# The output projection of the pooling channels as seven block products, inside the last attention pass of a transformer block on one NeuronCore

## The chip, the cores and the metric

The kernel runs on one core of a Trainium2 chip. The core has a matrix engine (PE; PEld is its loading of weights), a vector engine (DVE), an activation engine (ACT), GpSimd (POOL) and a queue engine (SP) which here issues nearly all transfers. The kernel puts PE's results into PSUM, in banks of 128 x 512 fp32 numbers, and all else into SBUF; GpSimd works on SBUF alone here. The metric is the time of one execution in device microseconds; a smaller number is better. Traces give, for one profiled execution, the start and the duration of every instruction.

## The reference, cut to what matters

```python
for layer in range(DEPTH):                                    # DEPTH = 1, S = D = 1024
    h = rmsnorm(x, norm1_g[layer])
    proj = h @ w_in[layer]                                    # q | k | v | f_logit | u
    attn = forgetting_attention(q, k, v, log_f)               # 8 heads x 64, causal: 512 channels
    pool = multiscale_pool(u, w_pool[layer], pool_scale[layer])   # 4 groups x 128: 512 channels
    mixed = concatenate([attn, pool], axis=-1)
    x = x + mixed @ w_out[layer]                              # the output projection, 1024 x 1024
    h2 = rmsnorm(x, norm2_g[layer])
    x = x + (silu(h2 @ w_gate[layer]) * (h2 @ w_up[layer])) @ w_down[layer]
return rmsnorm(x, final_g)
```

The output projection contracts over 1024 mixed channels, in eight chunks of 128: chunks 0 to 3 are the pairs of attention heads, chunks 4 to 7 the four pooling groups. All data is fp32. The kernel writes each operand as a high and a low part in a rounded fp32 format and computes a product as three matmuls (high x high, high x low, low x high).

## The kernel before, in words

**Stages.** First comes RMSNorm, the input projections and the pooling (to about 100 us in the trace), then four passes of attention over two heads each (to about 350 us), the last rows of the output projection with the second norm and its transposes (to about 410 us), then the gate and up products (to about 820 us) and the down products with the final norm. The gate, up and down products are already written as seven block products instead of eight.

**Attention with a filler.** `attend` (L711) runs one pass of eight jobs. A job is one head and two blocks of 128 queries; its steps are scores (`z`, L617 and L618), transposes of the scaled probabilities (`tp`, L643) and products with the values (`po`, L657). Scores are made one job ahead. ACT takes the exponential (L626), and GpSimd divides by the row sum (`p`, L629). Behind each step `attend` takes some steps from a generator, the filler, so that PE has other matmuls between those that wait for a softmax. In passes 0, 1 and 2 the filler is the projection of the next heads (`project`, `project_v23`); in pass 3 it is the output projection. The instructions are recorded in this order, and the framework's scheduler then sets each engine's own order; each engine runs its list strictly in order.

**The output projection before.** `first_rows` (L817) makes, for each of eight row blocks `tt` and each half of the columns, one PSUM group over chunks 4 and 5 (`rows2`, L803: six matmuls, then a DVE add into the row of x held in SBUF, L811). `second_rows` (L844) does the same over chunks 6, 7 and 0 (nine matmuls). Chunks 1, 2 and 3 come last (`last_row`, L873), when the last heads are done; chunk 3 is `mix_halves` (L859), which reads the last pair of heads back from DRAM in halves. Every chunk needs two pages, 128 x 1024 each: the mixed channels (`mixd` in DRAM, transposed) and the rows of `w_out`. A page is loaded (`raw_page`, L750, most into one of the two buffers `wr`), and split (`split`, L119): ACT writes the high part, DVE or GpSimd the low part. The groups use two PSUM banks with the tag `m` in turn. The rows of x are loaded whole, 128 x 1024 (`x2_load`, L794).

**Buffers that the change touches.** `vc` in `vpool` holds the pooled features of two groups (`pf01`, L505) until they are split, and values of the third head pair from pass 1 on. `va` holds values that the last job still reads, and takes the raw half pages of chunk 3. `hi` (two buffers of 128 x 512) serves `project`.

## Time and profile before

| what | value |
|---|---|
| time, median of 3 runs | 1035.73 us (1035.46 to 1036.53) |
| the profiled execution, first to last instruction (its own time is given as this span) | 1033.6 us |
| PE busy | 1024.3 us, 5104 matmuls |
| DVE, ACT, POOL busy | 632.8, 454.2, 381.1 us |
| mean granted TensorE clock | 0.998 |
| moved by DMA | 130.21 MB |

The span is what the trace covers; 2.1 us of the median lie outside it. A busy share of PE says little by itself, since consecutive matmuls overlap: the start-to-start distance of two matmuls is what one costs. In a row of a timeline stand the start and the duration in us, the engine, the line, the operation, the output and inputs, and the shapes. "o" is a PSUM group of the output projection, "r_mix" and "r_wo" are raw pages, "h_" and "l_" (or "hl_") their high and low parts.

### The profile page before, as it was taken

To read this page: it belongs to the slowest core of one execution; us is meant where nothing else is said; L and a number is where in the kernel's file an instruction comes from. 1 tells how busy PE (TensorE), PEld (TensorE's weight loads), DVE (VectorE), ACT (ScalarE), POOL (GpSimd) and SP (SyncE) were. 2 spreads that over 40 slices of the span, in tenths; PEclk is the share of its full clock that TensorE was granted. 3 is DMA by queue.
4 is the path that set the end of the run, shared out by engine and by line. 5 is a ranking of instruction groups with operands and counts; after the bars stand their busy time and mean duration, and the time that the engine had idled before them with its cause. 6 is when DMAs were issued, how large, how long until landed. Compare 5 with 4: busy or idle time off the path is not lost.

```text
span 1033.6 us, 14202 instructions
## 1 busy us (share of the span) xinstructions
PE 1024.3 (99%) x5104; PEld 868.9 (84%) x5104; DVE 632.8 (61%) x1000; ACT 454.2 (44%) x733; POOL 381.1 (37%) x312
## 2 busy tenths in 40 slices
PE   9999999999999999999999999999999999999997
PEld 7988888998888888888888888888888888888886
DVE  7565566776886479744433334334334789788886
ACT  7434355665665257533333233233233343333346
POOL 4350121213346043447537536636637510000045
PEclk9999999999999999999999999999999999999999
DMA  7224434333643134343143143143236755353424
GB/s 251 53 47 143 105 81 103 84 102 89 224 175 106 49 136 129 103 143 112 62 132 113 62 133 112 64 131 113 81 113 251 248 204 175 110 198 97 153 92 163
DMA packets 108439, 130.21 MB, mean 126 GB/s; under 512 B 7369, under 2 KB 70353, under 8 KB 108369
## 3 DMA queue, kind: packets, MB, share of 16 engines
q1 hardware_dynamic: 96544, 108.18, 33.4%
q10 hardware_dynamic: 11504, 20.47, 5.2%
q8 instruction: 40, 0.66, 0.2%
q0 software_dynamic: 320, 0.66, 0.2%
q14 instruction: 31, 0.25, 0.1%
HBM read 86.29 MB, written 33.03 MB: 115 GB/s over the span
## 4 chain that ended last, share of the span: by engine, by line
PE 98%; DMA 1%; ACT 0%; DVE 0%; POOL 0%; issue 0%; ACTq 0%; POOLq 0%
PE gu_P L161 14%; PE gu_P L162 14%; PE gu_P L163 14%; PE d L161 7%; PE d L162 7%; PE d L163 7%; PE po L657 4%; PE tp L643 3%; PE o L161 3%; PE o L162 3%; PE qk L161 3%; PE qk L162 3%; PE qk L163 3%; PE o L163 3%; PE v L374 2%; PE z L618 2%
## 5 line engine op out<-in xcount | busy, mean ns | idle before, releaser
L121 DVE TENSOR_TENSOR gu_P_l<-s,gu_P_h 128x1024 fp32r<-128x1024 f32 (+1 forms) x48 | 66.5, 1393 | 98.6 <-ACT gu_P_h L120 98.5
L162 PE MATMUL d<-d,d 128*128 128x512 f32 (+1 forms) x308 | 119.5, 388 | 0.0
L163 PE MATMUL d<-d,d 128*128 128x512 f32 (+1 forms) x308 | 119.5, 388 | 0.0
L629 POOL TENSOR_SCALAR p<-p,rr 128x128 f32<-128x128 f32 (+3 forms) x64 | 48.6, 764 | 175.5 <-DVE rr L628 140.2
L161 PE MATMUL d<-d,d 128*128 128x512 f32 x308 | 107.8, 388 | 0.0
L120 ACT ACTIVATE d<-r_f 128x1536 fp32r<-128x1536 f32 (+1 forms) x28 | 38.8, 1384 | 117.6 <-PE d L162 101.6
L121 DVE TENSOR_TENSOR gu_P_l<-r,gu_P_h 128x1024 fp32r<-128x1024 f32 x32 | 48.9, 1527 | 64.3 <-ACT gu_P_h L120 64.3
L1063 POOL TENSOR_TENSOR s<-r 128x1024 f32<-128x1024 f32 x10 | 24.0, 2401 | 161.9 <-DMA r<-in_w_up_dram 116.0
L120 ACT ACTIVATE gu_P_h<-r 128x1024 fp32r<-128x1024 f32 x32 | 33.8, 1060 | 91.1 <-PE gu_P L162 35.5
L162 PEld LDWEIGHTS d<-d,d 128*128 128x128 f32 x308 | 57.8, 188 | 12.0 <-DVE d L121 0.2
L161 PEld LDWEIGHTS d<-d,d 128*128 128x128 f32 x308 | 57.8, 188 | 12.0
L163 PEld LDWEIGHTS d<-d,d 128*128 128x128 f32 x308 | 57.8, 188 | 11.9
L626 ACT ACTIVATE p<-p,mn 128x128 f32<-128x128 f32 (+3 forms) x64 | 49.3, 772 | 32.8 <-DVE mn L620 29.9
L1291 POOL TENSOR_SCALAR sse<-sse 128x1 f32<-128x1 f32 x7 | 3.5, 494 | 158.1 <-ACT junk L1287 158.1
L1150 POOL TENSOR_TENSOR h<-h,qh 128x512 f32<-128x512 f32 x33 | 44.3, 1345 | 32.3 <-ACT qh L1148 24.1
L648 DVE TENSOR_TENSOR tl<-tp,th 128x512 fp32r<-128x512 f32 (+1 forms) x80 | 49.3, 632 | 10.7 <-ACT th L647 9.7
L120 ACT ACTIVATE gu_P_h<-s 128x1024 fp32r<-128x1024 f32 (+1 forms) x48 | 47.0, 984 | 19.7 <-PE gu_P L162 13.0
L1147 DVE TENSOR_TENSOR qh<-gu_P,sn_sU 128x512 f32<-128x512 f32 x22 | 15.2, 690 | 60.5 <-POOL h L1150 43.2
L121 DVE TENSOR_TENSOR d<-r_f,d 128x1536 fp32r<-128x1536 f32 (+1 forms) x28 | 45.7, 1633 | 10.5 <-ACT d L120 10.5
L163 PE MATMUL qk<-hTh,l_qk 128*128 128x512 f32 x128 | 50.7, 396 | 0.0
L161 PE MATMUL qk<-hTh,h_qk 128*128 128x512 f32 x128 | 50.6, 395 | 0.0
L162 PE MATMUL qk<-hTl,h_qk 128*128 128x512 f32 x128 | 50.4, 394 | 0.0
(337 smaller groups left out, 3067.1 us busy)
## 6 DMA issues: line engine op xcount, KB each, us to landing
r_f<-hsdP SPq DMA_DIRECT2D x77, 256.0 KB
r_wd<-in_w_down_dram SPq DMA_DIRECT2D x22, 512.0 KB
hsdP<-f ACTq DMA_DIRECT2D x43, 256.0 KB
r<-in_w_gate_dram SPq DMA_DIRECT2D x21, 512.0 KB
r<-in_w_up_dram SPq DMA_DIRECT2D x21, 512.0 KB
s<-hi SPq DMA_DIRECT2D x64, 128.0 KB
hsdP<-h ACTq DMA_DIRECT2D x32, 256.0 KB
x<-in_x_dram SPq DMA_DIRECT2D x8, 512.0 KB
```

The costliest lines, as they stand in the source:

```text
L120: mark["hi"] = nc.scalar.activation(out=hi, in_=src, func=AF.Copy)
L121: return eng.tensor_tensor(out=lo, in0=src, in1=f32(hi), op=ALU.subtract)
L161: nc.tensor.matmul(ps, lh, rh, start=start, stop=False, **kw)
L162: nc.tensor.matmul(ps, lh, rl, start=False, stop=False, **kw)
L163: mark["mm"] = nc.tensor.matmul(ps, ll, rh, start=False, stop=stop, **kw)
L626: nc.scalar.activation(out=pr[:, :n], in_=pr[:, :n], func=AF.Exp, scale=-1.0, bias=mn, accum_out=rs)
L629: nc.gpsimd.tensor_scalar(out=pr[:, :n], in0=pr[:, :n], scalar1=rr, scalar2=1.0, op0=ALU.mult, op1=ALU.mult)
L643: nc.tensor.transpose(tp[:, w : w + P], probs[h, 2 * sb + a][:, s * P : (s + 1) * P], ident)
L648: nc.vector.tensor_tensor(out=tl[:, :w], in0=tp[:, :w], in1=f32(th[:, :w]), op=ALU.subtract)
L657: mark["pv"] = nc.tensor.matmul(po[:, first * P : 2 * P], vt[p][:, s, j, :], part[:, o : o + wd], start=(s == 0 and part is th), stop=(s = ...
L1063: g(out=s1, in0=a21, in1=a22, op=ALU.add)
L1150: nc.gpsimd.tensor_tensor(out=h, in0=h, in1=q, op=ALU.mult)
```

## The change

The four pooling chunks (a contraction over 512) are taken as a 2 x 2 block product: 512 tokens by 256 channels, times 256 channels by 512 columns. Seven products of sums of blocks replace eight. The four sums on each side are made by GpSimd during passes 0 and 1 from `mixd` and `w_out` in DRAM and stored in DRAM again (`sumd`), in four rounds through the buffer `vc`: two loads of 512 KB, four subtractions or additions of 128 x 512, one store of 1 MB. `project_v23` first finishes what is left of these rounds.

In pass 3 the filler is `output_steps`: chunk 0 alone for four rows, then P2 with chunk 0, then P7 and P4, then P1, P6, P5 and P3, each for two token blocks in two PSUM banks. A chain of products keeps adding to its bank, and after each product DVE adds the running sum to the half row of x that it belongs to. Fourteen pages take the place of eight; three later pages (`LATE`) go through the two small buffers `hi` in halves, and rows of x are loaded in halves. A step has 6 or 9 matmuls as before; there are 30 steps instead of 32, and `attend` takes 25 of them instead of 27.

```diff
-    def project_v23():
+    def project_v23(side):
+        for _ in side:
+            pass
         vtile(2)
...
-    def attend(p, fill, counts, drain=True):
+    def attend(p, fill, counts, drain=True, side=iter(())):
...
                 for f in step:
                     f()
+                next(side, None)
                 want = quota * (k + 1) // len(steps)
...
+    rounds = [("wo", 0), ("wo", 1), ("mix", 0), ("mix", 1)]
+    def quarter_load(r):
+        kind, i = rounds[r]
+        t = quarters[r] = vpool.tile([P, 4, 512], F32, tag="vc", bufs=1, name=f"quarters{r}")
+        for k in range(2):
+            dst = t[:, 2 * k : 2 * k + 2, :].rearrange("p a e -> p (a e)")
+            nc.sync.dma_start(out=dst, in_=page_source(kind, NPAIR + 2 * k + i))
+    def quarter_sums(r):
...
+        for out, in0, in1, op in todo:
+            nc.gpsimd.tensor_tensor(out=out, in0=in0, in1=in1, op=op)
+            yield
+            yield
+    def quarter_store(r):
+        nc.sync.dma_start(out=sumd[rounds[r]], in_=quarters[r])
...
+    def part(ps, k, c, start, stop):
+        (ah, al), (bh, bl) = operands["mix", k], operands["wo", k]
+        for i in range(2):
+            ts, hs = slice(i * 512 + c * P, i * 512 + (c + 1) * P), slice(i * 512, (i + 1) * 512)
+            mm3(ps, ah[:, ts], al[:, ts], bh[:, hs], bl[:, hs], start and i == 0, stop and i == 1, True)
...
+    SPLITS = [
+        ("mix", "P2", M, G, -1), ("wo", "P2", O, V, 0), ("mix", "P7", M, G, 2), ("wo", "P7", O, V, 3),
+        ("mix", "P4", ST1, G, 5), ("wo", "P4", VC, V, 6), ("mix", "P1", M, G, 8), ("wo", "P1", O, V, 9),
+        ("mix", "P6", M, G, 12), ("wo", "P6", O, G, 13), ("mix", "P5", ST0, G, 14), ("wo", "P5", W, V, 15),
+        ("mix", "P3", ST1, G, 16), ("wo", "P3", VC, G, 18), ("wo", 1, O, V, 24), ("mix", 1, M, G, 24),
+        ("wo", 2, O, V, 26), ("mix", 2, M, G, 27), ("wo", 3, W, V, 30),
+    ]
...
+        def link(k, down, right, start, stop, more=False):
+            def do(c):
+                ps = fresh(f"o{k}", c) if start else held[c]
+                part(ps, k, c, start, stop and not more)
+                tt = c + down * NH
+                if more:
+                    whole(ps, tt, right, False, stop)
+                add_to(tt, right, ps)
...
+        order = [(alone, 0), (alone, 1)]
+        order += chain(("P2", 0, 0, True, True, True))
+        order += chain(("P7", 1, 1, True, False), ("P4", 1, 0, False, True, True))
+        order += chain(
+            ("P1", 0, 0, True, False), ("P6", 1, 0, False, False), ("P5", 1, 1, False, False),
+            ("P3", 0, 1, False, True, True),
+        )
...
-    attend(3, fill, [3, 3, 4, 4, 4, 4, 3, 2], drain=False)
+    attend(3, fill, [2, 3, 4, 3, 4, 4, 3, 2], drain=False)
```

In `SPLITS` the columns are the page, the destination, the engine of the low part (G is GpSimd, V is DVE) and the step ahead of which the split is recorded.

**Where the order moves, first place: GpSimd at the start of attention.** `p0_0` is the first head's first block of probabilities; `quarters0` and `quarters1` are the first two rounds of sums. Before:

```order
L432 DMA augd_101<-clo_831 8x1024
L432 DMA augd_101<-nlo_839 8x1024
L629 TENSOR_SCALAR p0_0_1205<-p0_0_1205,rr0_0_1213 128x128
L629 TENSOR_SCALAR p0_1_1216<-p0_1_1216,rr0_1_1224 128x256
L629 TENSOR_SCALAR p0_2_1258<-p0_2_1258,rr0_2_1266 128x384
```

And after:

```order
L432 DMA augd_101<-nlo_839 8x1024
L770 TENSOR_TENSOR quarters0_1240<-quarters0_1240 128x512 x4
L770 TENSOR_TENSOR quarters1_1479<-quarters1_1479 128x512 x3
L631 TENSOR_SCALAR p0_0_1209<-p0_0_1209,rr0_0_1217 128x128
L631 TENSOR_SCALAR p0_1_1220<-p0_1_1220,rr0_1_1228 128x256
L631 TENSOR_SCALAR p0_2_1265<-p0_2_1265,rr0_2_1273 128x384
L770 TENSOR_TENSOR quarters1_1479<-quarters1_1479 128x512
```

Seven sums stand ahead of the first scaling of probabilities; in SP's list the store of the first round and the loads of the second stand among the copies of the key stacks of the first heads.

**Second place: GpSimd in the second half of the last pass.** `p7_i` are the last head's blocks, `l_...` the low parts of pages. Before:

```order
L629 TENSOR_SCALAR p7_3_3963<-p7_3_3963,rr7_3_3971 128x512
L121 TENSOR_TENSOR hl_mix0_3900<-r_mix0_3666,hl_mix0_3900 128x1024
L121 TENSOR_TENSOR l_mix1_3983<-r_mix1_3980,h_mix1_3982 128x1024
L629 TENSOR_SCALAR p7_4_4044<-p7_4_4044,rr7_4_4057 128x640
L121 TENSOR_TENSOR l_wo2_3989<-r_wo2_3986,h_wo2_3988 128x1024
L121 TENSOR_TENSOR l_mix2_3995<-r_mix2_3992,h_mix2_3994 128x1024
L629 TENSOR_SCALAR p7_5_4094<-p7_5_4094,rr7_5_4107 128x768
L629 TENSOR_SCALAR p7_6_4150<-p7_6_4150,rr7_6_4163 128x896
L121 TENSOR_TENSOR l_wo3_4001<-r_wo3_3998,h_wo3_4000 128x1024
L629 TENSOR_SCALAR p7_7_4190<-p7_7_4190,rr7_7_4203 128x1024
```

After:

```order
L631 TENSOR_SCALAR p7_3_4042<-p7_3_4042,rr7_3_4050 128x512
L121 TENSOR_TENSOR l_mixP6_3996<-r_mixP6_3862,h_mixP6_3995 128x1024
L121 TENSOR_TENSOR l_woP6_4026<-r_woP6_3913,h_woP6_4025 128x1024
L631 TENSOR_SCALAR p7_4_4101<-p7_4_4101,rr7_4_4114 128x640
L121 TENSOR_TENSOR l_mixP5_4054<-r_mixP5_3999,h_mixP5_4053 128x1024
L631 TENSOR_SCALAR p7_5_4151<-p7_5_4151,rr7_5_4164 128x768
L121 TENSOR_TENSOR l_mixP3_4118<-r_mixP3_4057,h_mixP3_4117 128x1024
L121 TENSOR_TENSOR hl_woP3_4167<-r_woP3_4080,hl_woP3_4167 128x1024
L631 TENSOR_SCALAR p7_6_4204<-p7_6_4204,rr7_6_4217 128x896
L631 TENSOR_SCALAR p7_7_4243<-p7_7_4243,rr7_7_4256 128x1024
L121 TENSOR_TENSOR l_mix1_4370<-r_mix1_4170,h_mix1_4369 128x1024
L121 TENSOR_TENSOR l_mix2_4415<-r_mix2_0_4403,h_mix2_4414 128x512
```

The low parts of the pages of P6, P5 and P3 stand where those of chunks 0, 1, 2 and 3 stood, and chunks 1 and 2 come behind the last scaling.

**Third place: SP at the end of attention.** `at7_i` are results of the last head on their way to `mixd`. Before:

```order
L669 DMA mixd_100<-at7_2_4233 64x256
L865 DMA r_mix3_4326<-mixd_100 128x512
L669 DMA mixd_100<-at7_3_4311 64x256
L865 DMA r_mix3_4326<-mixd_100 128x512
L992 DMA r_gu0_P1_4428<-in_w_gate_dram 128x4x128
```

After:

```order
L671 DMA mixd_100<-at7_2_4285 64x256
L988 DMA r_mix3_4380<-mixd_100 128x512
L820 DMA r_mix2_0_4403<-mixd_100 128x512
L820 DMA r_mix2_1_4404<-mixd_100 128x512
L671 DMA mixd_100<-at7_3_4357 64x256
L988 DMA r_mix3_4380<-mixd_100 128x512
L820 DMA r_wo3_0_4420<-in_w_out_dram 128x512
L820 DMA r_wo3_1_4421<-in_w_out_dram 128x512
L1117 DMA r_gu0_P1_4494<-in_w_gate_dram 128x4x128
```

The loads of chunk 2's mixed page and of chunk 3's weights, which were issued during the pass before, stand between and behind the two loads of chunk 3's mixed page.

160 lines of the change are left out of this document (112 added, 48 removed).

## The prediction, made before the changed kernel was run

> **What bounds the kernel now.** I read the page first: busy shares, the chain, the granted clock.
>
> ```profile
> span 1033.6 us, 14202 instructions
> PE 1024.3 (99%) x5104; PEld 868.9 (84%) x5104; DVE 632.8 (61%) x1000; ACT 454.2 (44%) x733; POOL 381.1 (37%) x312
> PEclk9999999999999999999999999999999999999999
> PE 98%; DMA 1%; ACT 0%; DVE 0%; POOL 0%; issue 0%; ACTq 0%; POOLq 0%
> ```
>
> PE is the chain from end to end at an undiminished clock. But matmuls overlap, so a busy PE could still be waiting inside its durations. The busy times by stage, with the count of matmuls in brackets, and one stretch of the timeline settle that:
>
> ```profile
> core 0: us, PE busy (x) PEld busy (x) DVE busy (x) ACT busy (x) POOL busy (x), PEclk, DMA share, GB/s
> 270.00:275.00 5.00, 5.00 (x30) 4.38 (x29) 5.00 (x16) 3.31 (x7) 1.01 (x1) 1.00 1.02 381
> 275.00:300.00 25.00, 25.00 (x152) 22.21 (x152) 21.23 (x54) 15.97 (x33) 11.68 (x10) 1.00 0.67 235
> 300.00:325.00 25.00, 25.00 (x151) 22.00 (x149) 19.67 (x51) 18.80 (x36) 18.48 (x14) 1.00 0.37 116
> 425.00:800.00 375.00, 375.00 (x1656) 310.50 (x1655) 151.54 (x143) 127.79 (x168) 207.87 (x112) 1.00 0.35 116
> ```
>
> ```profile
> 282.47 0.51 PE L643 MATMUL tp<-ident,p 128*128 128x128 f32 x3
> 282.73 0.48 PE L161 MATMUL o<-h_wo,hl_mix 128*128 128x512 f32 x1
> 283.06 0.39 PE L162 MATMUL o<-l_wo,hl_mix 128*128 128x512 f32 x1
> 283.28 0.39 PE L163 MATMUL o<-h_wo,hl_mix 128*128 128x512 f32 x1
> ```
>
> In the gate and up stage 1656 matmuls take 375 us: one of 512 columns costs 0.2264 us start to start, though its duration reads 0.39. In the last attention pass the projection's matmuls start 0.22 to 0.23 us apart as well. Only the first after a group of transposes takes longer, 0.33 us (282.73 to 283.06), 0.10 more. So PE is at its own pace in the pass that is changed, and each matmul taken away is worth its 0.2264 us, as long as no operand is late. The question is then only what the change makes late.
>
> **The change, part by part.** I sum against the span, 1033.6; the 2.1 us by which the median exceeds it should stay.
>
> *Matmuls.* Chunks 4 to 7 took 4 chunks x 16 groups x 3 = 192 matmuls; seven products of 2 chunks x 4 token blocks x 3 make 168. 24 x 0.2264 = **-5.4 us**. The changed order also enters the projection's matmuls from transposes or scores 19 times instead of 27; at 0.10 us each that is up to -0.8. Not every entry need cost as much as the one shown, so I take **-0.3** and keep 0 and -0.8 as ends.
>
> *GpSimd's sums.* Four rounds of four operations. Nearest rows: an operation of the same size on GpSimd, and the idle time of GpSimd ahead of its first scaling.
>
> ```profile
> L1150 POOL TENSOR_TENSOR h<-h,qh 128x512 f32<-128x512 f32 x33 | 44.3, 1345 | 32.3 <-ACT qh L1148 24.1
> 115.55 1.49 POOL L629 TENSOR_SCALAR p<-p,rr 128x128 f32<-128x128 f32 x3 [38.96 <-DVE rr L628]
> ```
>
> 16 x 1.345 = 21.5 us, of which seven operations, 9.4 us, stand in the 39 us in which GpSimd idled. What they wait for is a chain through SP: load, four sums, store of the round, load of the next. Its start and what stands behind it:
>
> ```profile
> 93.80 1.22 DVE L121 TENSOR_TENSOR pl<-pf,ph 128x1024 fp32r<-128x1024 f32 x1
> 95.68 0.76 SPq L549 DMA_DIRECT2D s<-augd  x2
> 105.95 0.47 SPq L569 DMA_DIRECT2D s<-hi  x1
> 119.68 0.27 PE L643 MATMUL tp<-ident,p 128*128 128x128 f32 x1
> ```
>
> The buffer `vc` is free at 95.0, SP at 96.4. A load of 256 KB takes 2.4 to 3.0 us from issue to use (rows below, at the end of attention); 1 MB has 0.75 MB more at 381 GB/s (window 270:275), 2.0 us, so about 4.7. Load until 101.2, sums until 106.6, store until 111.3, second load until 116.0, three sums until 120.0, two scalings in 0.9 (the first three took 1.49): 120.9. The first transpose was at 119.68; the changed order puts seven more projection matmuls ahead of it, so it is due at 121.3. That fits by 0.4 us. The store also stands ahead of the key copies that were issued at 105.95; these slip by about 1 us, with the first scores moved back by the same 1.6. I take **+0.3** for the start; ends 0 and +3 (each of the three transfers 1 us slower). The later rounds meet probabilities that are scaled a whole job ahead: GpSimd waits for PE to free their buffers, not the reverse.
>
> ```profile
> POOL p L629 <- PE tp L643: 15.2, 3, 7.4
> ```
>
> *Pages of the last pass.* Fourteen pages for eight, three later ones in halves. Costs by group:
>
> ```profile
> L121 POOL TENSOR_TENSOR l_mix<-r_mix,h_mix 128x1024 fp32r<-128x1024 f32 x4 | 9.6, 2402 | 7.5 <-ACT h_mix L120 7.5
> L121 DVE TENSOR_TENSOR l_mix<-r_mix,h_mix 128x1024 fp32r<-128x1024 f32 x1 | 1.2, 1223 | 0.0
> L120 ACT ACTIVATE h_wo<-r_wo 128x1024 fp32r<-128x1024 f32 x6 | 6.3, 1058 | 2.6 <-DMA r_wo<-in_w_out_dram 2.6
> L811 DVE TENSOR_TENSOR x_r<-o,x_r 128x512 f32<-128x512 f32 x16 | 10.7, 680 | 4.1 <-PE o L163 4.1
> ```
>
> Of the six more pages' worth, three low parts go to GpSimd (7.2 us) and about three to DVE (3.7 us), and ACT gets 6 x 1.06 = 6.4 us at most. The windows leave 3.8 to 9 us idle in 25 on each, so on average there is room: **0**. The densest place is five low parts (12.0 us) and four scalings between the end of P7 and the first product of P3: there the changed order has 132 matmuls, 21.7 us at the 152 in 25 of the window. Six pages go through two raw buffers in that time; one takes load 2.4 + ACT 1.06 + GpSimd 2.4 = 5.9 us, two at a time 2.95, six 17.7. Slack 4.0 us.
>
> *Running sums in two banks.* PE may add to a bank again only after DVE's add has read it. With steps of six, the other bank's step gives 1.36 us; the add takes 0.68. Cover enough: **0**; if DVE is held by a page's low part (1.22), 0.5 us at a time. The 32 adds themselves are as many as before. The loads of x in halves carry the same bytes, behind fewer others: 0.
>
> *The end of attention.* Here the change puts transfers in series where before they were done. The rows of before, by engine:
>
> ```profile
> 349.85 0.28 PE L657 MATMUL po<-tl,v 128*128 128x128 f32 x1
> 358.21 0.39 PE L161 MATMUL o<-h_wo,h_mix 128*128 128x512 f32 x1
> 359.57 0.39 PE L161 MATMUL o<-h_wo,mix_h 128*128 128x512 f32 x1
> ```
>
> ```profile
> 350.16 0.33 SPq L865 DMA_DIRECT2D r_mix<-mixd  x1
> 351.03 0.87 SPq L669 DMA_DIRECT2D mixd<-at  x1
> 353.39 0.33 SPq L865 DMA_DIRECT2D r_mix<-mixd  x1
> ```
>
> ```profile
> 353.12 0.63 ACT L120 ACTIVATE mix_h<-r_mix 128x512 fp32r<-128x512 f32 x1 [2.57 <-DMA r_mix<-mixd]
> 355.83 0.63 ACT L120 ACTIVATE mix_h<-r_mix 128x512 fp32r<-128x512 f32 x1 [2.07 <-DMA r_mix<-mixd]
> ```
>
> ```profile
> 353.84 0.69 DVE L121 TENSOR_TENSOR mix_l<-r_mix,mix_h 128x512 fp32r<-128x512 f32 x1 [0.86 <-ACT mix_h L120]
> ```
>
> Call V the end of the last product with the values, 349.97 here. Before, 36 matmuls cover the loads of chunk 3 (last rows from V + 8.2, chunk 3 used at V + 9.6), whose first half is split by V + 4.6: 5 us of slack. After, 30 matmuls follow V, so the last rows start at V + 6.9 and want chunk 3's weights at V + 8.3. These are now late: SP's list is chunk 3 (V + 0.2), two halves of chunk 2 (V + 0.6, V + 1.0), the last result's store, chunk 3 again, then the two halves of the weights, which need the `hi` buffers that chunk 2 leaves. Chunk 3's first half can be split at V + 3.2 (350.16 to 353.12), chunk 2's behind it by V + 4.4 and V + 5.0 (0.63 each), GpSimd's low parts (half of 2.40) end at V + 5.6 and V + 6.8, the weights' first half is there 2.4 to 3.0 later, V + 8.0 to 8.6, its high part at V + 8.7 to 9.2. PE waits 0.4 to 0.9: **+0.6**. The second half's high part comes at V + 9.9 to 10.4, eight matmuls (1.8) after PE resumes at 8.9: in time. Ends: 0, if both loads are quicker by 0.4; +2.5, if each of the two loads in series takes 0.6 more and each of two low parts another 0.65. What is late next is nothing more: the second norm and its transposes follow the last rows as before.
>
> [...]
>
> ```profile
> 278.35 1.71 DVE L121 TENSOR_TENSOR l_wo<-r_wo,h_wo 128x1024 fp32r<-128x1024 f32 x1
> 276.57 2.40 POOL L121 TENSOR_TENSOR l_mix<-r_mix,h_mix 128x1024 fp32r<-128x1024 f32 x1 [3.24 <-ACT h_mix L120]
> 278.95 2.10 POOL L629 TENSOR_SCALAR p<-p,rr 128x1024 f32<-128x1024 f32 x1
> ```
>
> A DVE low part that usually takes 1.22 took 1.71 where it began inside a GpSimd low part that ended at 278.97, and the scaling behind it took 2.10. [...]
>
> **Sum.** -5.4 - 0.3 + 0.3 + 0.6 = -4.8: span 1028.8, median 1035.7 - 4.8 = **1030.9 us**.
>
> **Rivals.** *A. Attention's start comes late.* The chain of transfers through SP has 0.4 us to spare and seven sums ahead of the first scaling. For it: GpSimd and SP go strictly in order. Against: the scores themselves are moved back. At +1.5 to 3 instead of 0.3: 1032.1 to 1033.6.
>
> [...]
>
> *C. The filler was cover, not load.* The last pass loses 18 matmuls, 4.1 us, ahead of V; if the heads' own chain (score, exponential, scaling, transpose) cannot go faster, PE waits that long and the change does not give what it takes away: -5.4 - 0.3 + 0.9 + 4.1 = -0.7, 1035.0. Against it: probabilities lie a job ahead, and DVE and ACT have idle time in the windows.
>
> *D. Slower: the ring of two raw buffers.* Place: between the end of P7 and P3. If a page costs 5.2 us there instead of 2.95 (loads and splits hardly overlapping, as SP, ACT and GpSimd each go in order among stores, exponentials and scalings), six take 31.2 against 21.7, 9.5 us late: 1030.9 + 9.5 = 1040.4. It costs from 3.6 us a page and makes the kernel slower from 4.8. For it: GpSimd is 18.48 of 25 us busy there already. Against: with two buffers the transfers of one overlap the splits of the other, and DMA is at a share of 0.37 there.
>
> **How the numbers follow.** Forecast 0.56, A 0.12, B 0.12, C 0.11, D 0.09. The forecast's own range is 1029.8 (all stalls 0, -0.5 us of entries more or less) to 1032. I give **1029.3 to 1034.6**: it leaves out D, about half of C and a little below. Two runs of this kernel can be told apart at about 0.2%, 2.1 us: faster means below 1033.7, slower above 1037.8. Faster: 0.56 + 0.10 (A) + 0.10 (B) + 0.02 (C) = 0.78; slower: D, 0.09; same: the rest, 0.13.
>
> **What would show it.** PE's count falls to 5080, and in 425:800 nothing changes but the place. [...] A P3 product waiting for `hl_wo` by microseconds would show D. A gain above 6.2 us would show that I missed something that PE waited for before.

## The result and the profile after

The changed kernel takes 1044.95 us (1041.50 to 1046.48) against 1036.13 us (1035.46 to 1037.70) for the kernel before: a ratio of 1.0082 (95% interval 1.0062 to 1.0102). It is slower by 8.8 us, 0.8%, clear of the noise; the prediction had it 4.8 us faster.

The page of the changed kernel, its head, PE's clock and PE's waits:

```profile
span 1039.7 us, 14286 instructions
PE 1023.7 (98%) x5080; PEld 864.0 (83%) x5080; DVE 636.0 (61%) x1005; ACT 460.9 (44%) x742; POOL 410.5 (39%) x332
PEclk9999999999999999999999999999999999999999
```

```profile
PE po L659 <- DVE at L670: 1.5, 2, 1.2
PE o L161 <- ACT h_wo L120: 1.2, 1, 1.2
PE warm L254 <- DVE junk L252: 1.2, 1, 1.2
PE tr_a L150 <- DVE x L300: 0.9, 1, 0.9
PE qk L161 <- ACT p L628: 0.9, 1, 0.9
PE po L659 <- DVE tl L650: 0.8, 2, 0.5
PE oP L161 <- ACT h_woP L120: 0.7, 1, 0.7
PE oP L162 <- DVE hl_woP L121: 0.7, 1, 0.7
```

(In a row of waits stand the total in us, how often, and the longest.) PE's busy time fell by 0.6 us and its share by a point, which says nothing. The waits do: of these eight only the two at the very start (`warm`, `tr_a`) were in the kernel before, and the other six are in attention and at its end. The same by stage, busy us and matmuls:

```profile
core 0: us, PE busy (x) PEld busy (x) DVE busy (x) ACT busy (x) POOL busy (x), PEclk, DMA share, GB/s
275.00:300.00 25.00, 23.71 (x138) 20.13 (x137) 18.88 (x49) 15.42 (x31) 9.73 (x9) 1.00 0.78 261
300.00:325.00 25.00, 23.04 (x129) 19.54 (x128) 17.36 (x45) 16.33 (x34) 15.85 (x11) 1.00 0.42 130
325.00:350.00 25.00, 25.00 (x151) 21.94 (x150) 19.08 (x35) 14.49 (x26) 10.81 (x7) 1.00 0.37 117
350.00:375.00 25.00, 22.72 (x106) 17.56 (x105) 15.71 (x24) 9.38 (x17) 6.30 (x7) 1.00 0.40 132
425.00:800.00 375.00, 375.00 (x1656) 310.51 (x1655) 154.28 (x151) 131.12 (x173) 205.85 (x111) 1.00 0.34 111
```

From 425 us on nothing changed. In 275:325, where PE was at 25.00 twice before, it now stands still for 3.2 us. The program moves 141.76 MB by DMA, where it was 130.21.

I compared the start of every matmul with the start of the one ahead plus its own plain pace (0.2268 us for 512 columns), and added up what was over that, stretch by stretch. This is the account of the profiled execution against the one before:

| part of the program | forecast | measured, us |
|---|---|---|
| 24 matmuls fewer | -5.4 | -5.4 |
| small delays (under 0.15 us each) in the last pass | -0.3 | +1.1 |
| 60 to 265 us: sums, start of attention | +0.3 | +1.9 (one wait of 1.09 at 165.6) |
| 265 to 353 us: pages of the last pass | 0 | +6.0 (0.95 at 276; 3.9 at 296 to 306; 1.15 at 350 to 353) |
| 354 to 367 us: chunk 3's weights | +0.6 | +2.05 |
| second norm, start and end of the program | 0 | +0.5 |
| span | -4.8 | +6.1 |

The profiled execution itself took 1041.50 us, the lowest of the four. The three others took 1044.33 to 1046.48 at a mean granted clock of 0.996, 0.996 and 0.995, where the profiled one had 0.998; what that is comes at the end.

**The largest place, 296 to 306 us.** The timeline of the changed kernel: the buffer that GpSimd frees, the load that needed it, and what ACT does when the load is late.

```profile
295.91 2.38 POOL L121 TENSOR_TENSOR l_mixP<-r_mixP,h_mixP 128x1024 fp32r<-128x1024 f32 x1 [0.70 <-ACT h_mixP L120]
298.32 0.80 SPq L820 DMA_DIRECT2D r_mixP<-mixd  x2
301.75 1.06 ACT L120 ACTIVATE h_mixP<-r_mixP 128x1024 fp32r<-128x1024 f32 x1 [1.61 <-DMA r_mixP<-mixd]
302.84 0.38 ACT L669 ACTIVATE at<-po 64x256 f32<-64x256 f32 x1
303.24 1.06 ACT L120 ACTIVATE hl_woP<-r_woP 128x1024 fp32r<-128x1024 f32 x1
303.73 0.39 PE L659 MATMUL po<-th,v 128*128 128x256 f32 x1 [1.16 <-DVE at L670]
306.41 0.50 PE L162 MATMUL oP<-hl_woP,h_mixP 128*128 128x512 f32 x1 [0.67 <-DVE hl_woP L121]
```

The low part of P4's channels ends at 298.29, and only then can P1's channels be loaded into that raw buffer. ACT stands at the split of P1 until 301.75 with 1.61 us idle, though nobody needs P1 yet: behind it in ACT's list are the copy `at` and the split of P4's weights, and PE waits for both. Against PE's pace these two waits cost 2.2 of the 3.9 us. The rest is three shorter waits for DVE ahead of them (0.61, 0.40 and 0.33 us at 297 to 301) and smaller ones.

### The profile page after: what moved, and what is told of

It is laid out like the page before. It is cut to its first block, busy times and chain, and to the rows that moved or that the text cites. A ratio compares the mean times of both kernels' runs of the same rounds, so it can differ in the third digit from the quotient of the medians.

```text
span 1039.7 us, 14286 instructions
## 1 busy us (share of the span) xinstructions
PE 1023.7 (98%) x5080; PEld 864.0 (83%) x5080; DVE 636.0 (61%) x1005; ACT 460.9 (44%) x742; POOL 410.5 (39%) x332
## 2 busy tenths in 40 slices
DMA packets 114631, 141.76 MB, mean 136 GB/s; under 512 B 8056, under 2 KB 71040, under 8 KB 114048
## 4 chain that ended last, share of the span: by engine, by line
PE 90%; DVE 2%; DMA 2%; ACT 2%; issue 1%; POOL 1%; SPq 0%; POOLq 0%; ACTq 0%; DVEq 0%
PE gu_P L163 13%; PE gu_P L162 13%; PE gu_P L161 13%; PE d L162 7%; PE d L163 7%; PE d L161 7%; PE qk L161 3%; PE qk L162 3%; PE qk L163 3%; PE po L659 3%; PE tp L645 3%; PE v L374 2%; PE u L163 1%; PE u L161 1%; PE u L162 1%
```

## What a matmul of the filler is worth: two cuts in the kernel before

If the filler is load, taking 24 matmuls out of the kernel before must give 5.4 us wherever they stand; if it is cover, it gives less. I took them once from the start of the last pass, once from its second half.

```diff
-            yield from rows2(lhs, rhs, tt, "o4")
+            few = slice(1 if n < 4 else 0, None)
+            yield from rows2(lhs[few], rhs[few], tt, "o4")
```

> The kernel before, with 24 matmuls of the last pass left out: the first four row blocks are summed over chunk 5 alone instead of chunks 4 and 5 (pages, splits and all else as before). Theory 'the filler is load': 24 x 0.2264 = 5.4 us less than before, about 1030.5. Rival C, 'the filler was cover': the 4 us ahead of the end of attention come back as waits, about 1034.5.

```diff
-        for tt in ORDER:
-            yield from rows2(second["mix"], second["wo"], tt, "o6")
+        for n, tt in enumerate(ORDER):
+            few = slice(1 if n < 4 else 0, None)
+            yield from rows2(second["mix"][few], second["wo"][few], tt, "o6")
```

> The kernel before, again with 24 matmuls of the last pass left out, but from its second half: for the first four row blocks of the second list chunk 6 is left out of chunks 6, 7 and 0 (pages, splits and all else as before). Theory 'at the start of the last pass the transfers set the pace, later there is slack': 24 x 0.2264 = 5.4 us less than before, about 1030. Rival C, 'the filler is cover in the whole pass': waits take the place here too, within 1.5 us of before or slower, as in the fourth run.

At the start: 1038.26 us, ratio 1.0025 (1.0016 to 1.0035), so **slower** with 24 matmuls fewer. In the second half: 1031.17 us, 0.9958 (0.9943 to 0.9973), 4.3 us faster; there PE has no wait over 0.15 us from 255 to 388 us, and about 1.0 us is given back at 389, at the second norm. PE's waits of the first kernel, then its timeline on ACT:

```profile
PE z L617 <- DVE mn L620: 1.8, 1, 1.8
PE tp L643 <- POOL p L629: 0.9, 1, 0.9
PE tp L643 <- DVE tl L648: 0.6, 1, 0.6
PE tp L643 <- DVE rr L628: 0.5, 1, 0.5
```

```profile
277.39 1.06 ACT L120 ACTIVATE h_mix<-r_mix 128x1024 fp32r<-128x1024 f32 x1 [2.09 <-DMA r_mix<-mixd]
278.36 0.58 ACT L647 ACTIVATE th<-tp 128x512 fp32r<-128x512 f32 x1
278.83 0.60 ACT L626 ACTIVATE p<-p,mn 128x384 f32<-128x384 f32 x1
...
281.65 1.06 ACT L120 ACTIVATE h_wo<-r_wo 128x1024 fp32r<-128x1024 f32 x1 [0.94 <-DMA r_wo<-in_w_out_dram]
```

It is the mechanism seen above, in the kernel before. PE arrives earlier, the page does not; ACT waits 2.09 us for it, and behind that split stand the copy of a transpose and an exponential, so PE waits for the softmax. The DMA engines were busy nearly without a pause there already, in the kernel before:

```profile
265.00:270.00 5.00, 5.00 (x32) 4.51 (x31) 4.26 (x10) 3.44 (x7) 0.91 (x1) 1.00 0.94 304
270.00:275.00 5.00, 5.00 (x30) 4.38 (x29) 5.00 (x16) 3.31 (x7) 1.01 (x1) 1.00 1.02 381
275.00:280.00 5.00, 5.00 (x30) 4.44 (x30) 5.00 (x12) 4.87 (x13) 3.43 (x2) 1.00 1.00 315
280.00:285.00 5.00, 5.00 (x32) 4.46 (x31) 4.69 (x13) 1.99 (x5) 3.14 (x5) 1.00 0.66 193
285.00:290.00 5.00, 5.00 (x35) 4.58 (x34) 3.22 (x10) 3.09 (x5) 3.17 (x2) 1.00 1.02 410
290.00:295.00 5.00, 5.00 (x28) 4.18 (x28) 3.32 (x7) 2.14 (x6) 0.92 (x2) 1.00 0.62 245
295.00:300.00 5.00, 5.00 (x35) 4.55 (x34) 5.00 (x15) 3.90 (x6) 1.02 (x1) 1.00 0.05 13
```

From 265 to 290 four of five stretches have a DMA share of 0.94 to 1.02. The 25 us window that the prediction read, 275 to 300, averages 0.67: two of its stretches are at 1.00 and 1.02, and its last is nearly empty. So 24 matmuls taken from the second half of the pass are worth 4.3 us, 0.18 each, and only the second norm keeps them from their full 5.4. Taken from the start they are worth nothing: waits of 5.5 us at 270 to 285 take their place, and what makes the kernel slower than before is about 1.0 us at the second norm and a granted clock of 0.91 and 0.75 in 280:285 and 285:290, of which the last section tells.

## The pages

Two cuts in the changed kernel. In the first twelve loads are left out and the pages are split from P2's raw pages; in the second six pages are neither loaded nor split.

```diff
+        if isinstance(c, str) and c != "P2":
+            raw_pages[kind, c] = raw_pages["kept", kind]
+            return
```

> The changed kernel with the loads of the twelve pages of P7, P4, P1, P6, P5 and P3 left out: their splits are all made, but from the two raw pages of P2, which are there from the start (so the products are of other numbers; the rounds of sums stay). Theory 'the supply of raw pages through the ring of two buffers': the stalls at 296 to 305 (3.9 us) go, and perhaps that at 276 (0.95), so 1040 to 1041. Rival 'ACT, DVE and GpSimd have too much to split': the splits are all still there, the stalls stay, 1043.5 or more.

```diff
+        if isinstance(c, str) and c != "P2":
+            operands[kind, c] = operands[kind, "P2"]
+            return
```

> The changed kernel with the pages of P7, P4, P1, P6, P5 and P3 neither loaded nor split: their products take P2's operands (so the numbers are others; matmuls, adds, rows of x and the rounds of sums stay as they are). Theory 'the six products' pages, loaded and split beside attention, are what makes the last pass late': no stalls between 280 and 350, what remains is 1.5 us in the first passes, the wait at 276 and the 3 us around the end of attention, so 1036 to 1039, or less if no clock is halved. Rival 'the order of the matmuls itself (fewer of them between scores and values, adds after each product) is the cause': 1042 or more.

Both came out slower in total: 1051.19 us (1.0150; 1.0134 to 1.0165) and 1050.26 us (1.0141; 1.0121 to 1.0161). In the first the scheduler set splits, which no longer wait for a load, ahead of that of P2's own weights, whose load then comes late: ACT idles 4.35 us for it and PE waits 3.7 us (`h_woP`), so it settles nothing. In the second, what happens between 278 and 347 us can be read, and the end cannot: P2's operands now hold the buffers that chunks 2 and 3 need, and PE waits 3.0 us for `h_mix`. The stage in question:

```profile
300.00:325.00 25.00, 25.00 (x148) 22.05 (x147) 17.31 (x48) 11.22 (x26) 5.98 (x8) 1.00 0.11 32
```

Without the page work PE does 148 matmuls in 300:325 and never stands still, against 129 and 23.04 us in the changed kernel. From 277.6 to 347 us there is no stall over 0.15 us at all. The 3.9 us at 296 to 306 are therefore the price of the pages; the wait at 276 is still there (1.7 us).

**More raw buffers.** The next edit takes the ring away: P2's weights, P4's and P1's pages get raw buffers of their own among tiles that are unused by then, and are loaded earlier.

```diff
+    RAW["wo", "P2"] = lambda: op.tile([P, 1024], F32, tag="ol", bufs=2, name="r_woP2")
+    for (kind, c), (pl, tag, nb) in {
+        ("mix", "P4"): (wpool, "wh", 2), ("wo", "P4"): (wpool, "wl", 2),
+        ("mix", "P1"): (ap_, "st0", 6), ("wo", "P1"): (ap_, "st0", 6),
```

> The changed kernel with more raw buffers at the start of the last pass: the weights of P2 are loaded into a still unused buffer of the projection's own pages, P4's two pages into the second buffers for weights, P1's two pages into two buffers of finished key stacks; only the other nine go through the ring of two, and all of them are loaded earlier. Splits, sums and matmuls are unchanged. Theory 'page loads late, with attention's own work queued behind the waiting split on ACT': the stalls at 276 (0.95 in the first profile, 2.7 in two others) and at 296 to 305 (3.9) go, and with them the windows of halved clock that follow such stalls, so 1037 to 1040. Rival 'the splits themselves are too much for ACT, DVE and GpSimd': the waits come back a little later, 1043 or more.

1044.28 us, ratio 1.0082 (1.0065 to 1.0099): the same as the changed kernel. The stalls at 296 to 306 fell from 3.9 to 1.2 us, as they did in the best version below, which gives fewer pages a buffer of their own; so the ring made most of them. But 2.1 us came up earlier, at 273 to 276, where the early loads now stand ahead of the rows of x, and 1.55 us at 287, again for an add that waits for its half row of x. The timeline on DVE, and PE's clock (the third number from the end) in the window behind it:

```profile
272.89 0.69 DVE L895 TENSOR_TENSOR x_r<-o,x_r 128x512 f32<-128x512 f32 x1 [1.06 <-DMA x_r<-in_x_dram]
```

```profile
275.00:280.00 5.00, 4.20 (x15) 3.40 (x16) 4.72 (x16) 3.16 (x9) 1.34 (x2) 0.66 0.83 200
```

**Other orders.** Six further versions shift buffers, order or the issuing queue. In short:

The second step of chunk 0 taken last, with its rows of x loaded later:

```diff
-        order = [(alone, 0), (alone, 1)]
+        order = [(alone, 0)]
...
+        order += [(alone, 1)]
```

> The changed kernel with one edit in the order: of the two steps in which chunk 0 is multiplied alone, the second (rows 6 and 7) comes last instead of second, and the right halves of x for it are loaded later. Those two steps take 256 KB of x for every three matmuls, four times what P2's steps with nine matmuls for 256 KB take per matmul... in all 1 MB within 12 matmuls. Theory 'at the start of the last pass the transfers are the limit': with half of that put off, the stall ahead of P2's first matmuls (0.95, in two other executions 2.7, with windows of halved clock) gets shorter or goes, 1 to 3 us less than the changed kernel, 1042 to 1044. Rival 'P2's weights wait for their raw buffer alone': P2 is wanted one step earlier and its weights come when they came, the stall grows by the step's 1.4 us, 1046.

1048.55 us, 1.0124 (1.0107 to 1.0141): 2.0 us of stalls are left at 273 to 281, and the step, now at the end, meets the second norm, where some 8 us are lost.

The raw buffers above, with the low part of chunk 1's weights on GpSimd, chunk 3's weights early (below), and GpSimd issuing the stores of the sums:

```diff
-        nc.sync.dma_start(out=sumd[rounds[r]], in_=quarters[r])
+        nc.gpsimd.dma_start(out=sumd[rounds[r]], in_=quarters[r])
...
+        ("mix", "P3", ST1, G, 16), ("wo", "P3", VC, G, 18), ("wo", 1, O, G, 24), ("mix", 1, M, G, 24),
```

> The kernel of the run before, and three more edits: the low part of chunk 1's weights on GpSimd instead of DVE (so that it is not made beside GpSimd's low part of chunk 1's mixed page), chunk 3's weights loaded early as in the third run, and the stores of the sums issued by GpSimd itself instead of SP. Theory 'each stall has its own cause and they add': another 1.15 (350 to 353), 2.0 (362 to 367) and 1.1 (166) less, 1033 to 1036, at the level of the kernel before or under it. Rival 'what is won ahead of the second norm is given back there, since DVE is busy 41 of 45 us in that stage': 1036 to 1038, with waits of PE for DVE's add at 380 to 405.

1047.85 us, 1.0119 (1.0101 to 1.0138). The wait at 350 to 353 is gone. But attention starts late: the second round's loads go out at 113.67 us, where they did at 111.68, the first scaling begins at 122.57, where it did at 120.36, and PE waits 1.0 us for a copy of keys and 0.8 us for a scaling. How the change of queue delayed the loads was not traced.

The raw buffers, the lone step last, rows of x first, and the raw pages of chunks 2 and 3 in buffers of the probabilities:

```diff
+                ts = [
+                    ap_.tile([P, (n0 + i + 1) * P], F32, tag=f"pr{n0 + i}", bufs=1, name=f"r_{kind}{c}_{i}")[:, 0:512]
+                    for i in range(2)
+                ]
```

> The more raw buffers of the fifth run, but x first: the second lone step of chunk 0 last, as in the run before, the halves of x for the first steps loaded ahead of P7's and P4's pages; chunk 1's weights split by GpSimd; chunk 2's raw mixed page and chunk 3's raw weights in buffers of probabilities that are done before attention ends; the last round's store of sums ten steps later in the program. Theory 'late transfers, with attention's own work queued behind them, are all there is': none of the stalls of 0.5 us or more between 260 and 365, and no halved clock; 24 matmuls less against what is left at the second norm: 1031 to 1034. Rival 'the filler was cover, and its 18 matmuls ahead of the end of attention cannot be saved': waits of about 4 us spread over scores, transposes and values, 1035 to 1037.

1044.98 us, 1.0085 (1.0068 to 1.0102), with 13 us of stalls: again one of 1.1 us at 168, one of 1.65 us at 277 to 279 for P2's weights and one of 2.2 us at 364 to 366, and the rest at new places.

The best of the orders gives raw buffers only to P2's weights and P1's pages, puts x for the first steps ahead of P7's pages, moves chunk 1's low part to GpSimd and loads chunk 3's weights early:

```diff
+    RAW["wo", "P2"] = lambda: op.tile([P, 1024], F32, tag="ol", bufs=2, name="r_woP2")
+    for kind in ("mix", "wo"):
+        RAW[kind, "P1"] = lambda n=f"r_{kind}P1": ap_.tile([P, 1024], F32, tag="st0", bufs=6, name=n)
...
-        0: [(0, 0), (1, 0)], 1: [(2, 0), (3, 0)], 5: [(4, 0), (5, 0)], 7: [(6, 0), (7, 0)],
+        1: [(2, 0), (3, 0)], 5: [(4, 0), (5, 0)], 7: [(6, 0), (7, 0)],
```

> The changed kernel with three raw pages moved (P2's weights into the projection's own unused buffer, P1's two pages into finished key stacks, loaded while the transfers idle at 260), the halves of x for the first steps loaded ahead of P7's pages, chunk 1's weights split by GpSimd, chunk 3's weights loaded early as in the third run. Theory 'each stall has its own cause': the waits at 276 (0.95 to 2.7), 302 to 305 (2.3), 350 to 353 (1.15) and 362 to 367 (1.6) go, 1036 to 1038. Rival 'what PE gains it waits for at the next late transfer': 1041 or more.

1039.28 us, 1.0039 (1.0024 to 1.0053): by the ratios 4.5 us better than the changed kernel, and still slower than the kernel before. 5.9 us of stalls are left, most of them in four places: 1.09 at 165.7, 1.94 at 274 to 276, 1.2 at 297 to 302, 1.3 at 360. On this version a plain page was then loaded in one transfer and several steps were reordered,

```diff
-        order = [(alone, 0), (alone, 1)]
-        order += chain(("P2", 0, 0, True, True, True))
+        order = [(alone, 0)] + chain(("P2", 0, 0, True, True, True)) + [(alone, 1)]
```

> The kernel of the run before, with four edits of order: chunk 0's second lone step behind P2's steps instead of ahead of them; pages that are plain pieces of one matrix loaded by one transfer instead of two; the second half of chunk 3's mixed page split behind the last adds of the last pass; the last round's store of sums behind the key copies on SP. In the trace of the run before 5.9 us of stalls are left: 1.1 at 166 (SP waits for that store), 1.9 at 274 to 276 (DVE waits for a half of x, then the low part of P2's weights), 1.2 at 297 to 302, 1.3 at 360 (DVE's add stands behind that split). Theory 'order alone': those at 166, 274 and 360 go, 1035 to 1036.5. Rival 'each gain is given back at the next late transfer': 1038 or more.

which gave 1047.53 us, 1.0098 (1.0078 to 1.0117), with 18.5 us of stalls, most of them at new places. And on the best version with chunk 3's late half (below), 1039.57 us, GpSimd issued the first six half rows of x,

```diff
-    def half_load(tt, hf):
-        nc.sync.dma_start(out=x2_half(tt, hf), in_=xf[tt * P : (tt + 1) * P, hf * 512 : (hf + 1) * 512])
+    def half_load(tt, hf, queue=nc.sync):
+        queue.dma_start(out=x2_half(tt, hf), in_=xf[tt * P : (tt + 1) * P, hf * 512 : (hf + 1) * 512])
```

> The kernel of the thirteenth run with one edit: the first six halves of x (1.5 MB) are issued by GpSimd, which idles around 265, and no longer by SP, where they and P2's weights stand between and behind the key copies. In the thirteenth run's trace PE waits 2.2 us at 273 to 276, for DVE's add, which waits for a half of x, and for the low part of P2's weights behind it; in the fourteenth the same place is followed by two windows of halved clock. Theory 'SP, in order, brings x and P2's weights too late': those 2.2 us go, with the halved clock that sometimes follows, 1036 to 1037.5. Rival 'the transfers themselves are at their limit there, whoever issues them': within 1 us of the thirteenth run, 1038.5 or more.

which gave 1040.17 us, 1.0047 (1.0032 to 1.0063). In its profile the wait at 274 shrank to 0.2 us, and one of 1.24 us stood at 272.8 and two of 0.68 and 0.81 us at 293 to 295 in its place. DVE again waits there for a half row of x, 1.86 us until 271.07. Who issues the loads made no difference; this fits a limit in the transfers themselves, which no run tested alone.

## The sums

Taken out of the changed kernel (the pooling products then use plain pieces of the pages), and put alone into the kernel before, which makes no use of them:

```diff
-    side = side_steps()
+    side = iter(())
```

> The changed kernel without the four rounds of sums: their 8 loads, 16 GpSimd operations and 4 stores are left out, and the pages that held sums are loaded, at the same size and in the same halves, from plain pages instead (so seven products are still made, of other numbers). In the trace of the changed kernel the stalls of PE in passes 0 and 1 come to 1.5 us (0.4 at the first transposes, 1.1 at 165.6). Theory 'the pages of the last pass are the cost': 1.5 us less than the changed kernel, about 1043.4, and the stalls of the last pass and of the end stay. Rival 'the rounds of sums through SP and GpSimd are the cost, and the profiled execution happened to show little of it': at least 4 us less, 1041 or below.

```diff
+    sumd = {(kind, i): dram.tile([P, 4, 512], F32, name=f"sumd_{kind}{i}") for kind in ("mix", "wo") for i in range(2)}
+    rounds = [("wo", 0), ("wo", 1), ("mix", 0), ("mix", 1)]
...
-    attend(0, project(1), [5, 4, 4, 3, 8, 6, 6, 0])
-    attend(1, both(project(2), project_v23()), [10, 7, 6, 8, 10, 8, 12, 0])
```

> The kernel before, and the four rounds of sums in it, whose results nothing reads. Theory 'the rounds cost 1.1 to 1.5 us by themselves': 1036.6 to 1037. Rival 'the rounds are hidden where nothing else is late': within 0.4 us of before. Rival 'the rounds, their transfers too, cost more': 1038 or more.

Without sums the changed kernel took 1042.97 us, 1.0070 (1.0053 to 1.0087): the waits at 113 to 121 and at 166 were gone, and P2's wait at 274 grew to 2.7 us. By the ratios that is 1.2 us less than with sums, within the noise of these two. The sums alone cost the kernel before 2.0 us: 1037.68 against 1035.66 us, 1.0016 (1.0006 to 1.0025). The same cut in the best version (with chunk 3's late half, below) gave the same size:

> The kernel of the run above without the four rounds of sums (left out as in the first run: pages of other numbers at the same size). Theory 'the rounds cost what PE shows at 120 and 166': 1.1 to 1.5 us less than the run above, about 1036.7. Rival 'the rounds cost more than these waits show': 3 us less or more, 1035 or below.

1036.79 us, 1.0008 (0.9999 to 1.0018), 2.8 us less than with sums. The time that was expected, 1036.7, came out by luck: it was reckoned from 1038 for the version with sums, which took 1039.57, and the difference of 2.8 us is nearer to the rival's. So where they can be told from the noise the sums cost 2.0 to 2.8 us, not 0.3. The start of attention is the smaller part: in the changed kernel its first transpose came at about 121 us, as forecast, with 0.15 us of waiting, and in the kernel before with sums 0.6 us are lost there. GpSimd of that kernel at the fourth round of sums, then DVE and PE at the larger wait, 1.1 us against PE's pace:

```profile
152.26 4.02 POOL L770 TENSOR_TENSOR quarters<-quarters 128x512 f32<-128x512 f32 x3 [2.50 <-DMA quarters<-mixd]
156.25 0.92 POOL L631 TENSOR_SCALAR p<-p,rr 128x768 f32<-128x768 f32 x1
```

```profile
165.86 1.41 DVE L575 SCALAR_TENSOR_TENSOR s<-qk,hi 64x512 fp32r<-64x512 f32 x2
167.42 0.47 PE L161 MATMUL qk<-hTh,h_qk 128*128 128x512 f32 x1 [0.88 <-ACT p L628]
```

The scaling of the sixth block, at 152.41 us before, runs at 156.25: it was not "scaled a whole job ahead". My theory was that this delay makes the wait at 166. I put the last round's sums behind the scalings of the sixth and seventh blocks (on the version in which GpSimd issues x):

```diff
+                with tc.issue_after(mark["scaled", 1, 5 if any(out is q for q in (q3, q1)) else 6].ins):
+                    nc.gpsimd.tensor_tensor(out=out, in0=in0, in1=in1, op=op)
```

> The kernel of the run above with one more edit: of the last round's sums GpSimd makes two behind the scaling of the sixth block of probabilities of the second head and two behind that of the seventh, no longer three ahead of the one and one ahead of the other. In the fifteenth run, before with the sums alone, the scaling of that sixth block starts at 156.25 behind three sums (4.02 us) that waited for their load; in the kernel before it starts at 152.41. Theory 'a scaling stands behind sums that wait for their load': the 1.1 us of PE at 165 go, 1.0 to 1.5 us less than the run above, 1034.5 to 1036.5, at before or under it. Rival 'the sums are late then, and their store stands in the way elsewhere': no gain, or slower.

1039.23 us, 1.0038 (1.0027 to 1.0050). The scaling was back at 152.50 us, and the wait stayed at 1.1 us: the theory fell. What the timelines show is that with sums the last block's scores (their second half) start at 159.46 us on PE instead of 155.93, with 30 filler matmuls instead of 14 between them and the seventh block's; ACT then works without a pause from 161.1 us on. The bank that PE wants is read last by the two copies `s<-qk,hi` on DVE, which stand behind softmax work and end at 167.27; PE goes on 0.15 us later, as it does behind the same copies in the changed kernel and in this last version. (The view names an exponential of ACT, which doesn't touch that bank; it ends at about the same time.) That the scheduler's order of PE is the cause is a reading, and was not tried.

## The end of attention

Chunk 3's weights get the free half of `va` as raw buffer instead of `hi`, and are loaded behind the first half of chunk 3's channels:

```diff
+        if (kind, c) == ("wo", 3):
+            ts = [raw_pages["va"][:, 1, i * 512 : (i + 1) * 512] for i in range(2)]
```

> The changed kernel with the weights of chunk 3 loaded at the end of attention into the free second half of the buffer that holds chunk 3's raw mixed page, behind the first half of that page, and no longer into the two small buffers that chunk 2 leaves. Theory 'the loads in series at the end of attention': PE's wait for h_wo at 362 to 364 (1.25 us) and the 0.3 us behind it go, about 1.5 to 2 us less than the changed kernel, 1043.0 to 1043.5. Rival 'another load is then last there': within 0.5 us of the changed kernel.

1044.13 us, 1.0077 (1.0060 to 1.0093). The wait at 362 us went from 2.05 to 0.22; 2.6 us of new waits stand at the second norm, 384 to 404, for DVE. The wait and its loads in the changed kernel:

```profile
354.29 0.33 SPq L988 DMA_DIRECT2D r_mix<-mixd  x1
360.51 1.58 SPq L820 DMA_DIRECT2D r_wo<-in_w_out_dram  x2
362.58 0.63 ACT L120 ACTIVATE mix_h<-r_mix 128x512 fp32r<-128x512 f32 x1 [2.89 <-DMA r_mix<-mixd]
363.31 0.63 ACT L120 ACTIVATE h_wo<-r_wo 128x512 fp32r<-128x512 f32 x1
363.99 0.50 PE L161 MATMUL o<-h_wo,mix_h 128*128 128x512 f32 x1 [1.25 <-ACT h_wo L120]
```

V, taken as in the prediction (the start of the matmul behind the last product with the values), is 354.10. The weights' first half is issued at V + 6.4, where the prediction's list had V + 5.6, and by its queue's semaphore in the trace it lands at 363.23, V + 9.1, where the list had V + 8.0 to 8.6. ACT has just ended the split of chunk 3's second half then, at 363.21, so that split cost nothing: the load itself is late. In the best version another thing held PE at this place: DVE's add stood behind a split of chunk 3's second half. I put that split behind the last adds:

```diff
+    with tc.issue_after(mark["added"].ins):
+        split(*late_half[0])
```

> The kernel of the eleventh run with one edit: on DVE the second half of chunk 3's mixed page is split behind the last adds of the last pass, no longer ahead of them. In the eleventh run's trace PE waits 1.13 us at 360 for such an add, which stands behind that split, which waits for its transfer. Theory 'an add stands behind a split that waits for a transfer': that wait goes, 1.0 to 1.3 us less than the eleventh run, about 1038. Rival 'it is given back at the second norm, where DVE has no room': within 0.5 us of the eleventh run.

1039.57 us, 1.0038 (1.0025 to 1.0051), no gain on 1.0039: the wait at 360 fell from 1.3 to 0.4 us, and one at the second norm took its place, in this row of its timeline:

```profile
395.93 0.50 PE L161 MATMUL o<-h_wo,h_mix 128*128 128x512 f32 x1 [1.30 <-DVE x_s L884]
```

The kernel before in that stage:

```profile
365.00:410.00 45.00, 45.00 (x232) 37.79 (x231) 40.91 (x57) 30.59 (x55) 17.75 (x23) 1.00 0.42 141
```

DVE is busy 40.91 of 45 us there, and PE just does not wait. What PE gains at 360 it gives back here.

## Why the prediction was wrong

**"Each matmul taken away is worth its 0.2264 us, as long as no operand is late."** The count and the pace were right: 5080 matmuls, -5.4 us, 425:800 as before. The condition failed at the start of the last pass. I read the room on the engines from windows of 25 us and made no term of the DMA share in my own rows, 1.02 in 270:275; in four of the five stretches of 265:290 it was 0.94 or more, and the cut at that place (+2.2 us where -5.4 was due) shows that the filler there covers loads. V agrees: with 18 matmuls fewer ahead of it, it was due 4.1 us earlier than 349.97, and it came 4.1 us later. Rival C named this ("the filler was cover, not load"), for the heads' own chain; here the chain is late because a split ahead of it waits for a page.

**"The windows leave 3.8 to 9 us idle in 25 on each, so on average there is room: 0."** This is the step that failed most, 6.0 us. The engines did have room. But a split that waited for its load held up what stood behind it on ACT, whatever the average. The page work costs 3.9 us at 296 to 306, of which the wait of ACT for P1 makes 2.2; behind its split stood a copy of the heads' results and the split of P4's weights (in the kernel before with 24 matmuls less, the softmax). Another 0.95 us is P2's weights, issued at 270.37 and split at 275.78, 5.4 us later, where the sum for the ring took 2.4 for a load. The last 1.15 us is DVE beside GpSimd (below). Rival D had the right ring of two buffers. Its place was between P4 and P1 instead of behind P7, its form one wait of ACT and a few short ones instead of an even shortage over six pages, its price 3.9 instead of 9.5 us. It came nearest to what happened, at a chance of 0.09. Without this term the account above would still end at +0.1 us: the gain of 5.4 was used up by the other terms, and the pages made it a loss.

**Entries, -0.3.** Counted by the number of changes from transposes to filler, which fell; the small delays in the last pass rose by 1.1 us, most of it between products with the values; why was not traced.

**Sums, +0.3.** The start of attention was right in the changed kernel, and rival A did not happen there. The step that failed is "the later rounds meet probabilities that are scaled a whole job ahead": the sixth block's scaling ran 3.8 us later. But setting it right did not take the wait away, so the 2.0 to 2.8 us are measured and their path is open, but for the two places where PE waits (0.6 and 1.1 us in the kernel before with sums).

**End of attention, +0.6 (0 to 2.5).** The mechanism, chunk 3's weights late by loads in series, was right, and 2.05 is within the ends and where rival B, the end of attention at +2 to 2.5, had it, by the loads (0.8 us later out and 2.7 on the way). The 0.65 us for each of two low parts in the upper end is an estimate that no run shows: a low part on DVE beside one on GpSimd took 0.49 us more than alone in the kernel before (1.71 against 1.22), and 1.34 more in the changed one, at the place that follows below.

**"What is late next is nothing more".** Wrong: the second norm, 0.47 us here, and up to 2.6 us once PE gets there earlier.

**DVE beside GpSimd.** A place that I had not named: the low part of chunk 1's weights. The rows of the changed kernel:

```profile
347.33 2.39 POOL L121 TENSOR_TENSOR l_mix<-r_mix,h_mix 128x1024 fp32r<-128x1024 f32 x1 [9.40 <-ACT h_mix L120]
348.23 2.58 DVE L121 TENSOR_TENSOR l_wo<-r_wo,h_wo 128x1024 fp32r<-128x1024 f32 x1 [1.12 <-ACT h_wo L120]
350.83 0.43 DVE L670 TENSOR_TENSOR at<-po,at 64x256 f32<-64x256 f32 x1
351.31 0.38 PE L659 MATMUL po<-th,v 128*128 128x256 f32 x1 [0.37 <-DVE at L670]
```

DVE took 2.58 us where the four low parts `l_woP` took 1.24 on average, the copy behind it came late, and PE lost 1.15 us. With this low part on GpSimd the loss was gone, in the best version for one. DVE's instruction began inside GpSimd's and ended 1.09 us after it (349.72 and 350.81); in the prediction's rows of the kernel before it is 1.09 us as well (278.97 and 280.06). What holds DVE there, no run shows.

**Not settled.** The wait at 165.6 us; the growth of the small delays; and the 2.8 to 5.0 us by which the three other executions of the changed kernel are above the profiled one. Their lower clocks can only be read by analogy with the profiles below. In the traces of the two versions nearest to the changed kernel (without sums, and with chunk 3's weights early) the wait for P2's weights is 2.7 us instead of 0.95, which may be the rest.

## What to carry to other kernels

Before a saving of matmuls is counted, take the same number out of the kernel before at the place in question: if that gains nothing, the matmuls there are cover. Read DMA shares in stretches as short as one page takes to load: the 25 us that averaged 0.67 held two of five stretches at 1.00 and 1.02. On an engine that runs its list in order, the price of a page that is late is what stands behind its split, and not the split: here 2.2 of the 3.9 us.

## What was not expected of the hardware: half clock after short waits

In several of these profiles the granted clock falls in the middle of the program, behind waits of PE. The kernel with 24 matmuls less at the start shows it in its windows, PEclk (a mean over the 5 us) being the third number from the end:

```profile
280.00:285.00 5.00, 1.73 (x9) 1.09 (x8) 2.88 (x6) 4.01 (x8) 5.00 (x6) 0.91 0.97 375
285.00:290.00 5.00, 5.00 (x27) 4.67 (x26) 4.73 (x12) 1.24 (x4) 2.45 (x2) 0.75 1.03 413
```

PE works 1.73 of 5 us, and then the clock is lower: the 0.09 and 0.25 that the two windows lack are 1.7 us of work, lost a second time. The rows of PE show the slow stretch. From 285.25 to 286.96 its products with the values, 128 x 256, start 0.21 us apart, where they start 0.12 us apart in the best version (349.75 to 350.47); from 287.58 on the projection's matmuls start 0.23 us apart, as elsewhere. The lowest clock of any window is 0.50, in 1030:1033 of the kernel before and in 1036:1039 of the changed one, both behind the last matmul. If it was 0.50 here too, 1.7 us of work are an estimated 3.4 us of half clock, from 284.1 to 287.5.

Others show the same. With more raw buffers PE works 4.16 of 5 us in 270:275, with a wait of 0.83 us following, and the clock is 0.66 in 275:280: again 1.7 us of work. In the version without sums and with chunk 3's late half PE works 3.16 of 5 us in 270:275, and the clock is 0.55 and 0.77 in the next two windows: 3.4 us of work. With the lone step last PE stands still for 1.36 and 3.01 us ahead of 405.05 and 408.56, and at 410.75 to 411.61 its matmuls start 0.43 us apart, where 0.2264 is the pace. But the clock did not always fall: in the changed kernel without sums P2's wait was 2.7 us, and the mean clock of that execution is 0.998, that of the kernel before; in the changed kernel PE works 3.72 of 5 us in 300:305, and the clock stays at 1.00 there and in 305:310. What decides it was not shown.

The profiled executions of the kernel before and of the changed one are at 1.00 in every window up to their last matmuls, at 1027 and 1033 us. A mean clock of 0.996 or 0.995 instead of 0.998 over 1040 us is 2 or 3 us of work, one or two times the 1.7 us above; by this estimate it would account for half to three quarters of the 2.8 to 5.0 us by which the three other executions of the changed kernel are above the profiled one.
